# Chunk decays of a state-space mixer: one product with ones for all chunks, instead of one read of a broadcast tile per chunk

## The chip, the cores and the metric

The kernel runs on one core of a Trainium2 chip. The time is the device time of one execution in microseconds (us), and the time before is the median of three executions. A profile is one further execution, recorded by the hardware profiler; its span, from the first to the last recorded instruction, is a little shorter than the time of that execution.

A core has five engines that run side by side, each with its own queue of instructions that it works off in order: TensorE (PE in the profile; its weight loads are listed apart as PEld), VectorE (DVE), ScalarE (ACT), GpSimd (POOL) and SyncE (SP), which here only issues DMA transfers. An instruction waits on semaphores for what it needs, and everything behind it on its engine waits with it.

## What is computed

One layer of a hybrid decoder on 1024 tokens with 16 learned meta tokens ahead of them, width 1024. Three mixers work in parallel on the same normalised input (stick-breaking attention, a Mamba-2 state-space mixer, latent attention), their outputs go through one output product, and a SwiGLU feed-forward block follows. The change touches only the state-space mixer, and in it the decays. Its part of the reference:

```python
X = (xh * dt[..., None]).reshape(b, nc, BLOCK, G, J, P)
dA = (dt * a).reshape(b, nc, BLOCK, G, J)
Acs = jnp.cumsum(dA, axis=2)
...
decay = jnp.exp(Acs[:, :, -1:] - Acs)
states = jnp.einsum('bclgn,bclgjp->bcgjpn', Bc, X * decay[..., None])
chunk_decay = jnp.exp(Acs[:, :, -1])

def step(carry, inp):
    cd, st = inp
    return carry * cd[..., None, None] + st, carry
...
y_off = jnp.einsum('bclgn,bcgjpn->bclgjp', Cc, prev) * jnp.exp(Acs)[..., None]
```

There are 16 heads in two groups of 8. The tokens fall into 9 chunks: chunk 0 holds the 16 meta tokens, chunks 1 to 8 hold 128 tokens each. For every chunk and head, `chunk_decay` is the exponential of the sum of dA over the chunk, and `decay` is the exponential of that sum less the running sum at each token.

## The kernel before

All operands are float32, but most products are taken as three products of a rounded part and a rest (`hi`, `lo`). The kernel is one long stream of such products: input projections and stick-breaking attention come first, with the convolution units of the state-space mixer between the heads; then the state-space chunks (the SSD stage) together with the latent projections; then latent attention, the gate units, the output product and the feed-forward block. The order of instructions on each engine isn't that of the text: the program is built with `TileContext(nc, schedule_with_timeline_sim=True)`, so a planner lays it down beforehand by a simulated timeline, starting from the order of the text, from marks such as `tc.high_priority` and from `tc.issue_after`. Work of independent parts is interleaved in this way: while the SSD stage runs, TensorE also gets the dense products of the latent projections (L145 to L147 in `dense_fm`, and L896 to L898).

**Where the running sums are made.** `running_sums` (L465) is called once, early in the second pair of attention heads. One product of the upper-triangular `tri` with `d1` (= dt·a, 128 tokens by 9 chunks × 16 heads) gives the running sums of all chunks at once (L468); VectorE copies them into `AT` (L469). Three rounds of transposes then turn them into rows (`acs`) that are stored in device memory as `s_sum` [9 chunks, 16 heads, 128 tokens], by SP (L479 for chunk 0, L482 for the others).

**Where they are used.** `ssd_chunk(c)` (L751) is called for c = 0 to 8. It loads `bc` (L756) and `xs` (L757) through SP, transposes `xs` and multiplies it by dt on the way out of PSUM (`X`, L769, VectorE). Then, for each of the two groups of 8 heads:

- SP loads `R` [128, 8, 128]: each head's row of running sums, copied to all 128 partitions (L786). The pool keeps 4 such tiles.
- ScalarE makes `cd`, the chunk decay, from the last column of `R` (L788); VectorE subtracts `AT` from that last column into `dec` (L789), and ScalarE takes its exponential (L799). Chunk 8 needs neither, as no state follows it.
- For c > 0, ScalarE makes `ea` (L793, two instructions) and `L` (L795, eight instructions, and L804) from `R`; VectorE multiplies `L` by the masked product of B and C (`cbm`, L808; L809).
- GpSimd multiplies `X` by `dec` into `Xd` (L800); TensorE makes the new state contribution `sps` from it (L817); GpSimd multiplies the state `S` by `cd` (L821) and VectorE adds `sps` (L824).
- TensorE makes `yo` from the old state (L813) and `yd` from `L` and `X` (L829). VectorE multiplies `ea` by `yo` (L814), GpSimd adds it to `y` (L834), VectorE adds `yd` (L835).

The tiles of this stage lie in the pool `p2`, which takes over space that stick-breaking attention used before; `AT`, `DT` and `tri` lie in `keep`, which lives longer. Other instructions that the text below meets: the eviction `lat` of a latent unit (L529), its squares and their sum (L517, L518), and the split of a weight in `load_w` (L132 on ScalarE, L134 on GpSimd).

Of the kernel before, what the change touches and what calls it, by code (L numbers as in the profile page):

```python
# [11 lines left out]
F32 = mybir.dt.float32  # L12
F32R = mybir.dt.float32r
BF16 = mybir.dt.bfloat16
AF = mybir.ActivationFunctionType
ALU = mybir.AluOpType
# [7 lines left out]
META = 16  # L24
# [35 lines left out]
def tile_hybrid_block(ctx: ExitStack, tc: tile.TileContext, a: dict):  # L60
    nc = tc.nc
    act, dve, pool, pe, sp = nc.scalar, nc.vector, nc.gpsimd, nc.tensor, nc.sync
# [36 lines left out]
    s_sum = dram.tile([9, 16, 128], F32, name="s_sum")  # L99
# [8 lines left out]
    ones = const.tile([128, 128], F32, name="ones")  # L108
# [71 lines left out]
    tp = tp_st.enter_context(tc.tile_pool(name="tp", bufs=2, space=PSUM))  # L180
# [6 lines left out]
    keep = hn_stack.enter_context(tc.tile_pool(name="keep", bufs=1))  # L187
    AT = keep.tile([128, 9, 16], F32, name="AT")
# [228 lines left out]


    dx = keep.tile([128, 9 * 16], F32, name="dx")

    def step_sizes():
        NC = 9 * 16
# [42 lines left out]
    def running_sums(d1):  # L465
        NC = 9 * 16
        pt = tp.tile([128, 512], F32, tag="tp", name="acum")
        pe.matmul(pt[:, :NC], tri, d1, start=True, stop=True)  # L468
        dve.tensor_copy(AT.rearrange("p b h -> p (b h)"), pt[:, :NC])  # L469

        for i, (t0, n) in enumerate(CH_ALL):
            acs = fill_tile("craw" if i == 2 else "cacc", "acs")[:16]
            pt = tp.tile([128, 512], F32, tag="tp", name="acst")
            for b in range(3 * i, 3 * i + 3):
                b0, w = BLOCKS[b]
                pe.transpose(pt[:16, b0 - t0 : b0 - t0 + w], AT[:w, b, :], ident[:w, :w])
            act.copy(acs[:, :n], pt[:16, :n])
            if i == 0:
                sp.dma_start(s_sum[0, :, :META], acs[:, :META])  # L479
            nb = min(3, n // 128)  # L480
            src = acs[:, n - 128 * nb : n].rearrange("h (b t) -> h b t", b=nb)
            sp.dma_start(s_sum[3 * i + 3 - nb : 3 * i + 3].rearrange("b h t -> h b t"), src)  # L482
# [166 lines left out]
    for i, (q0, qn) in enumerate(((0, 256), (256, 384), (640, 384))):  # L649
        c0, n = CH_ALL[i]  # L650
# [91 lines left out]
    with ExitStack() as st:  # L742
        la = st.enter_context(tc.tile_pool(name="la", bufs=1, side="right", reuse_waits="tile"))
        p2_st = ExitStack()
        p2 = p2_st.enter_context(tc.tile_pool(name="p2", bufs=2, side="right", reuse_waits="tile"))
        yps = st.enter_context(tc.tile_pool(name="yps", bufs=4, space=PSUM, reuse_waits="tile"))
        dsk = p2.tile([128, 8], F32, bufs=1, name="dsk")
        sp.dma_start(dsk, a["d_skip"])
        S = [p2.tile([128, 512], F32, bufs=1, name=f"S{g}") for g in range(2)]

        def ssd_chunk(c):  # L751
            n = META if c == 0 else 128
# [10 lines left out]
            for g in range(2):  # L763
                gs = slice(512 * g, 512 * (g + 1))
                hs = slice(8 * g, 8 * g + 8)
                pt = tp.tile([128, 512], F32, tag="tp", name="xtp")
# [11 lines left out]
            for g in range(2):  # L778
                gs = slice(512 * g, 512 * (g + 1))
                hs = slice(8 * g, 8 * g + 8)  # L780
                cd = p2.tile([128, 8], F32, tag="cd", name="cd")
                dec = p2.tile([128, 8], F32, tag="dec", name="dec")
                L = p2.tile([128, 8, 128], F32, tag="L", name="L")
                ea = p2.tile([128, 4, 128], F32, tag="yt", bufs=1, name="ea")
                R = p2.tile([128, 8, 128], F32, tag="R", bufs=4, name="R")
                sp.dma_start(R[:, :, :n], s_sum[c, hs, :n].partition_broadcast(128))  # L786
                if c < 8:
                    act.activation(cd, R[:, :, n - 1], AF.Exp)  # L788
                    dve.tensor_tensor(dec[:n], R[:n, :, n - 1], AT[:n, c, hs], op=ALU.subtract)  # L789
                if c > 0:  # L790
                    for e in range(2):
                        half = slice(64 * e, 64 * e + 64)
                        act.activation(ea[half], R[half, e::2, :], AF.Exp)  # L793
                    for h in range(8):
                        act.activation(  # L795
                            L[:, h, :], R[:, h, :], AF.Relu, scale=-1.0, bias=AT[:, c, 8 * g + h : 8 * g + h + 1]
                        )
                if c < 8:
                    act.activation(dec[:n], dec[:n], AF.Exp)  # L799
                    pool.tensor_tensor(  # L800
                        heads(Xd[:n, gs]), heads(X[:n, gs]), dec[:n].unsqueeze(2).to_broadcast([n, 8, 64]), op=ALU.mult
                    )
                if c > 0:
                    act.activation(L, L, AF.Exp, scale=-1.0)  # L804
                    pcb = tp.tile([128, 512], F32, tag="tp", name="cbp")
                    pe.matmul(pcb[:, :128], bc[:, g, :], bc[:, 2 + g, :], start=True, stop=True)
                    cbm = p2.tile([128, 128], F32, tag="cbm", name="cbm")
                    dve.tensor_tensor(cbm, pcb[:, :128], tri, op=ALU.mult)  # L808
                    dve.tensor_tensor(L, L, cbm.unsqueeze(1).to_broadcast([128, 8, 128]), op=ALU.mult)  # L809
                    yo = yps.tile([128, 512], F32, tag="y", name="yo")  # L810
                    for j in range(4):
                        ts = slice(128 * j, 128 * (j + 1))
                        pe.matmul(yo[:, ts], S[g][:, ts], bc[:, 2 + g, :], start=True, stop=True)  # L813
                    dve.tensor_tensor(ea, ea, yo.rearrange("p (j t) -> p j t", j=4), op=ALU.mult)  # L814
                if c < 8:
                    sps = yps.tile([128, 512], F32, tag="y", name="sps")
                    pe.matmul(sps, btok[:n, g * 128 : (g + 1) * 128], Xd[:n, gs], start=True, stop=True)  # L817
                    if c == 0:
                        dve.tensor_copy(S[g], sps)
                    else:  # L820
                        pool.tensor_tensor(  # L821
                            heads(S[g]), heads(S[g]), cd.unsqueeze(2).to_broadcast([128, 8, 64]), op=ALU.mult
                        )
                        dve.tensor_tensor(S[g], S[g], sps, op=ALU.add)  # L824
                if c > 0:
                    yd = yps.tile([128, 512], F32, tag="y", name="yd")
                    for h in range(8):
                        hh = 8 * g + h
                        pe.matmul(  # L829
                            yd[64 * (h % 2) : 64 * (h % 2) + 64, 128 * (h // 2) : 128 * (h // 2 + 1)],  # L830
                            X[:, hh * 64 : (hh + 1) * 64], L[:, h, :], start=True, stop=True,
                        )
                    yg = y[:, 4 * g : 4 * g + 4]
                    pool.tensor_tensor(yg, yg, ea, op=ALU.add)  # L834
                    dve.tensor_tensor(yg, yg, yd.rearrange("p (j t) -> p j t", j=4), op=ALU.add)  # L835
# [82 lines left out]
        for c0, n in CH_SHORT:  # L918
            c = slice(c0, c0 + n)
# [839 lines left out]
```

## Time and profile before

| | |
|---|---|
| median of 3 runs | 1741.38 us (1738.69 to 1743.46) |
| the profiled execution | 1737.8 us |
| its span | 1736.0 us |
| SSD stage in it | about 465 to 592 us |

In a row of the groups of instructions stand the line, the engine, the operation, what it writes and reads with the shapes, the count, and then: busy us in total, mean ns of one, and the idle time of the engine just before them with what ended most of it. In the timeline a row begins with the start and the length in us, and the bracket at its end says how long the engine had been idle and on what it had waited. In the view of waits the numbers are the total in us, how many times, and the longest.

### The profile page before, as it was taken

How to read it: one execution, taken by the hardware profiler on the slowest of the kernel's cores; microseconds unless marked ns; L12 is line 12 of the kernel's file. 1: busy time of each engine (PE TensorE's matmuls, PEld its weight loads, DVE VectorE, ACT ScalarE, POOL GpSimd, SP SyncE). 2: the span in 40 equal slices, each digit the busy share in tenths (PEclk: the TensorE clock that was granted, in tenths of full speed). 3: DMA queues.
4: the chain of work that ended last, by engine and by line, in shares of the span. 5: the costliest groups of instructions: out<-in, count | busy, mean ns of one | idle time of the engine just before them, and what ended most of it. 6: DMA issues, size and time to landing. Idle time of an engine off the chain costs nothing.

```text
span 1736.0 us, 26095 instructions
## 1 busy us (share of the span) xinstructions
PE 1681.3 (97%) x9529; PEld 1471.2 (85%) x9529; DVE 1154.7 (67%) x1726; ACT 844.6 (49%) x1763; POOL 735.3 (42%) x525
## 2 busy tenths in 40 slices
PE   8899999999998999999999999999999999999998
PEld 7889999999987789998888878778888888878887
DVE  7677568778587544556576556966666666688644
ACT  7465466556577627776454325422222322343333
POOL 3544335243578447563231445635554555200012
PEclk9999999999999999999999999999999999999999
DMA  4222222122566655348222352222322233999602
GB/s 164 72 73 66 82 81 88 39 83 71 173 213 170 211 203 153 113 122 285 62 80 75 94 178 73 71 100 92 113 93 97 93 101 110 329 395 370 234 1 97
DMA packets 150133, 230.90 MB, mean 133 GB/s; under 512 B 27043, under 2 KB 86597, under 8 KB 150005
## 3 DMA queue, kind: packets, MB, share of 16 engines
q1 hardware_dynamic: 130608, 213.67, 38.1%
q10 hardware_dynamic: 19396, 15.56, 3.0%
q8 instruction: 75, 1.23, 0.3%
q14 instruction: 54, 0.43, 0.1%
HBM read 166.07 MB, written 63.10 MB: 132 GB/s over the span
## 4 chain that ended last, share of the span: by engine, by line
PE 72%; DVE 7%; DMA 6%; issue 2%; POOL 2%; ACT 1%; SPq 1%; DVEq 0%; ACTq 0%; POOLq 0%
PE d_ps L145 8%; PE d_ps L147 8%; PE d_ps L146 8%; PE b_ps L1269 7%; PE b_ps L1271 7%; PE b_ps L1270 7%; PE b_ps L1554 2%; PE b_ps L1555 2%; PE b_ps L1553 2%; PE ptg L326 2%; DMA raw<-in_w_down_dram 1%; PE pv L305 1%; PE ptg L328 1%; PE pv L304 1%; PE sc_ps L979 1%
## 5 line engine op out<-in xcount | busy, mean ns | idle before, releaser
L145 PE MATMUL d_ps<-hnh,whi 128*128 128x384 f32 (+6 forms) x744 | 246.5, 331 | 3.6 <-DVE KS L607 2.4
L147 PE MATMUL d_ps<-hnl,whi 128*128 128x384 f32 (+6 forms) x744 | 246.6, 331 | 0.0
L146 PE MATMUL d_ps<-hnh,wlo 128*128 128x384 f32 (+6 forms) x744 | 245.8, 330 | 0.0
L134 POOL TENSOR_TENSOR wlo<-wraw,whi 128x1024 fp32r<-128x1024 f32 (+1 forms) x57 | 137.3, 2408 | 200.7 <-ACT whi L132 200.2
L145 PEld LDWEIGHTS d_ps<-hnh,whi 128*128 128x128 f32 (+1 forms) x744 | 140.1, 188 | 7.8 <-ACT vs L582 1.7
L147 PEld LDWEIGHTS d_ps<-hnl,whi 128*128 128x128 f32 (+1 forms) x744 | 140.1, 188 | 3.1 <-issue 0.8
L146 PEld LDWEIGHTS d_ps<-hnh,wlo 128*128 128x128 f32 (+1 forms) x744 | 140.1, 188 | 2.3
L1270 PE MATMUL b_ps<-T,wl 128*128 128x512 f32 x352 | 139.1, 395 | 1.3 <-POOL wl L1101 1.3
L1271 PE MATMUL b_ps<-T,wh 128*128 128x512 f32 x352 | 138.7, 395 | 1.3 <-DVE T L1101 1.3
L1269 PE MATMUL b_ps<-T,wh 128*128 128x512 f32 x352 | 139.1, 396 | 0.0
L312 DVE TENSOR_TENSOR pl<-ptg,ph 128x512 fp32r<-128x512 f32 (+1 forms) x160 | 99.8, 628 | 53.1 <-ACT ph L311 51.9
L696 DVE TENSOR_TENSOR_SCAN cm<-cm,sb_mask 128x144 f32<-128x144 f32 (+3 forms) x64 | 107.5, 1687 | 29.1 <-issue 18.8
L1100 ACT CAST op<-raw 128x1024 fp32r<-128x1024 f32 x69 | 71.1, 1050 | 110.3 <-PE d_ps L1555 65.4
L1101 DVE TENSOR_TENSOR op<-raw,op 128x1024 fp32r<-128x1024 f32 x69 | 84.1, 1229 | 40.5 <-ACT op L1100 40.4
L311 ACT CAST ph<-ptg 128x512 fp32r<-128x512 f32 (+1 forms) x160 | 85.6, 542 | 44.2 <-PE ptg L328 23.4
L132 ACT CAST whi<-wraw 128x1024 fp32r<-128x1024 f32 (+1 forms) x57 | 58.8, 1032 | 68.8 <-PE d_ps L147 35.1
L1101 POOL TENSOR_TENSOR wlo<-raw,whi 128x1024 fp32r<-128x1024 f32 x18 | 45.0, 2499 | 109.7 <-ACT whi L1100 109.7
L1101 POOL TENSOR_TENSOR wl<-raw,wh 128x512 fp32r<-128x512 f32 x46 | 75.5, 1648 | 30.2 <-ACT wh L1100 30.2
L1107 POOL TENSOR_TENSOR tt<-tt 128x512 f32<-128x512 f32 (+1 forms) x8 | 8.1, 1015 | 187.6 <-ACT tt L1625 187.4
L1104 DVE TENSOR_TENSOR raw<-raw 128x512 f32<-128x512 f32 x58 | 58.5, 1016 | 42.0 <-DMA raw<-in_w_gate_dram 37.3
L1100 ACT CAST wh<-raw 128x512 fp32r<-128x512 f32 x88 | 53.2, 616 | 65.9 <-PE b_ps L1271 65.8
L1270 PEld LDWEIGHTS b_ps<-T,wl 128*128 128x128 f32 x352 | 66.5, 189 | 17.3 <-POOL wl L1101 1.6
(431 smaller groups left out, 5117.8 us busy)
## 6 DMA issues: line engine op xcount, KB each, us to landing
raw<-in_w_down_dram SPq DMA_DIRECT2D x99, 256.0 KB, 5.3
s_hops<-gs SPq DMA_DIRECT2D x63, 256.0 KB, 2.0
raw<-s_hops SPq DMA_DIRECT2D x63, 256.0 KB, 5.4
raw<-in_w_gate_dram SPq DMA_DIRECT2D x22, 512.0 KB, 3.7
raw<-in_w_up_dram SPq DMA_DIRECT2D x22, 512.0 KB, 4.3
R<-s_sum SPq DMA_DIRECT2D x16, 512.0 KB, 4.7
wraw<-in_w_o_dram SPq DMA_DIRECT2D x16, 512.0 KB, 3.7
wraw<-in_w_xbc_dram SPq DMA_DIRECT2D x12, 512.0 KB, 4.0
```

The costliest lines, as they stand in the source:

```text
L134: pool.tensor_tensor(lo[:, :cols], raw[:, :cols], f32(hi[:, :cols]), op=ALU.subtract)
L145: pe.matmul(ps[:m, :n], wh, mh, start=(kt == 0), stop=False)
L146: pe.matmul(ps[:m, :n], wl, mh, start=False, stop=False)
L147: pe.matmul(ps[:m, :n], wh, ml, start=False, stop=(kt == nkt - 1))
L311: act.copy(ph[:, :n], pt[:, :n])
L312: dve.tensor_tensor(pl[:, :n], pt[:, :n], f32(ph[:, :n]), op=ALU.subtract)
L696: dve.tensor_tensor_scan(rev, rev, sb_mask[:, T - n_all :][:, ::-1], 1.0, ALU.mult, ALU.max)
L1100: act.copy(hi, value)
L1101: eng.tensor_tensor(lo, value, f32(hi), op=ALU.subtract)
L1269: pe.matmul(banks[j], hi[:, ks], UH[u][k], start=start and k == 0, stop=False, skip_group_check=skip)
L1270: pe.matmul(banks[j], lo[:, ks], UH[u][k], start=False, stop=False, skip_group_check=skip)
L1271: pe.matmul(banks[j], hi[:, ks], UL[u][k], start=False, stop=stop and k == 3, skip_group_check=skip)
```

## The change

The sum over each chunk is no longer read from the last column of the broadcast tile. `running_sums` makes it for all chunks at once with a product of a matrix of ones with `d1` (every partition then holds the same sum), and puts beside it that sum less the running sums. At the start of the SSD stage one exponential makes all chunk decays and all decays to the chunk's end (`decay`), and `cd` and `dec` become views of it. Chunk 0 then needs no `R`, so its two loads and the store of its row go; `R` keeps 3 tiles instead of 4. `SUMS` and `decay` take 1152 bytes of each partition.

```diff
+    SUMS = keep.tile([128, 2, 9 * 16], F32, name="SUMS")
...
         dve.tensor_copy(AT.rearrange("p b h -> p (b h)"), pt[:, :NC])
+        pt = tp.tile([128, 512], F32, tag="tp", name="asum")
+        pe.matmul(pt[:, :16], ones[:META], d1[:META, :16], start=True, stop=True)
+        pe.matmul(pt[:, 16:NC], ones, d1[:, 16:], start=True, stop=True)
+        dve.tensor_copy(SUMS[:, 0], pt[:, :NC])
+        pool.memset(SUMS[:, 1, :16], 0.0)
+        for rows, c in ((slice(0, META), slice(0, 16)), (slice(0, 128), slice(16, NC))):
+            dve.tensor_tensor(
+                SUMS[rows, 1, c], SUMS[rows, 0, c], AT.rearrange("p b h -> p (b h)")[rows, c], op=ALU.subtract
+            )
...
             act.copy(acs[:, :n], pt[:16, :n])
-            if i == 0:
-                sp.dma_start(s_sum[0, :, :META], acs[:, :META])
...
+        decay = p2.tile([128, 2, 9, 16], F32, bufs=1, name="decay")
+        act.activation(decay.rearrange("p e b h -> p e (b h)"), SUMS, AF.Exp)
...
-                cd = p2.tile([128, 8], F32, tag="cd", name="cd")
-                dec = p2.tile([128, 8], F32, tag="dec", name="dec")
+                cd, dec = decay[:, 0, c, hs], decay[:, 1, c, hs]
...
-                R = p2.tile([128, 8, 128], F32, tag="R", bufs=4, name="R")
-                sp.dma_start(R[:, :, :n], s_sum[c, hs, :n].partition_broadcast(128))
-                if c < 8:
-                    act.activation(cd, R[:, :, n - 1], AF.Exp)
-                    dve.tensor_tensor(dec[:n], R[:n, :, n - 1], AT[:n, c, hs], op=ALU.subtract)
                 if c > 0:
+                    R = p2.tile([128, 8, 128], F32, tag="R", bufs=3, name="R")
+                    sp.dma_start(R, s_sum[c, hs].partition_broadcast(128))
...
                 if c < 8:
-                    act.activation(dec[:n], dec[:n], AF.Exp)
                     pool.tensor_tensor(
```

## The prediction

> **What bounds the kernel now.** First the page's head and its busy line, then the table of windows around the one stretch that uses the changed tiles (columns: window, length, busy us and count of TensorE, its weight loads, VectorE, ScalarE, GpSimd, then granted clock, DMA share, GB/s).
>
> ```profile
> span 1736.0 us, 26095 instructions
> PE 1681.3 (97%) x9529; PEld 1471.2 (85%) x9529; DVE 1154.7 (67%) x1726; ACT 844.6 (49%) x1763; POOL 735.3 (42%) x525
> ...
> 465.00:592.00 127.00, 118.35 (x856) 98.14 (x856) 94.28 (x121) 101.72 (x255) 95.23 (x68) 0.97 0.66 199
> ...
> 530.00:540.00 10.00, 7.42 (x50) 5.63 (x47) 7.67 (x11) 8.73 (x25) 9.60 (x8) 0.83 0.75 213
> ...
> 550.00:560.00 10.00, 7.64 (x66) 6.16 (x61) 8.36 (x10) 6.84 (x18) 10.00 (x8) 0.94 0.67 175
> 560.00:570.00 10.00, 10.00 (x71) 8.04 (x70) 6.22 (x11) 8.57 (x24) 7.62 (x7) 0.89 0.46 136
> ```
>
> TensorE is busy 97% of the span, so a change pays only where TensorE stands idle. The SSD stage is 465 to 592 us. There TensorE is idle 127 − 118.35 = 8.65 us, and its clock was granted below full in three slices: 10 × (0.17 + 0.06 + 0.11) = 3.4 us lost. The other three engines are 74 to 80% full, each waiting for the others in a ring. The ring's waits touching the change, in the view of waits for 460 to 600 us, the lines of that stage, and the tile view of dec (min/median/max ns):
>
> ```profile
> ACT dec L799 <- DVE dec L789: 15.4, 9, 4.1
> ...
> L788 ACT ACTIVATE cd<-R 128x8 f32<-128x8 f32 x16 | 3.3, 209 | 2.9 <-POOL S L821 1.6 <-DMA R<-s_sum 1.0
> ...
> L789 DVE TENSOR_TENSOR dec<-R,AT 128x8 f32<-128x8 f32 x14 | 10.5, 750 | 2.8 <-POOL Xd L800 2.7
> ...
> L799 ACT ACTIVATE dec<-dec 128x8 f32<-128x8 f32 x14 | 2.9, 204 | 13.2 <-DVE dec L789 13.2
> ...
> L809 DVE TENSOR_TENSOR L<-L,cbm 128x1024 f32<-128x1024 f32 x16 | 30.6, 1911 | 1.1 <-ACT L L804 0.8
> ...
> L789 DVE TENSOR_TENSOR dec<-R,AT x16: 147/840/1039, 470.8 to 558.3; 128x8 f32<-128x8 f32 x14, 16x8 f32<-16x8 f32 x2
> ```
>
> ScalarE stands 15.4 us waiting for a subtraction of 8 columns that needs 0.15 us at best and takes 0.84 us at the median. So dec is an expensive trifle, but its price to the kernel is only what reaches TensorE.
>
> **The change, part by part.**
>
> *Removed in the stage.* ScalarE loses the 16 cd of 0.209 us (3.3 us) and 16 dec exponentials of about 0.2 us (3.2 us), and the 15.4 us of waiting. VectorE loses the 16 subtractions, some 10.8 us. GpSimd's Xd (L800) now needs only X; before it also needed the R load, L789 and L799. All are off TensorE, so I follow each idle piece of TensorE back in the timeline:
>
> ```profile
> 470.97 0.31 ACT L799 ACTIVATE dec<-dec 16x8 f32<-16x8 f32 x2 [2.18 <-DVE dec L789]
> 471.18 0.45 ACT L529 COPY lat<-d_ps 128x384 f32<-128x384 f32 x1
> 471.69 0.44 PE L145 MATMUL d_ps<-hnh,whi 128*128 128x384 f32 x1 [1.01 <-ACT lat L529]
> ...
> 488.19 2.04 POOL L821 TENSOR_TENSOR S<-S,cd 128x512 f32<-128x512 f32 x1
> ...
> 489.25 1.00 DVE L789 TENSOR_TENSOR dec<-R,AT 128x8 f32<-128x8 f32 x1
> ...
> 490.99 1.10 PE L817 MATMUL sps<-Xd,btok 128*128 128x512 f32 x2 [0.59 <-DVE ea L814]
> ...
> 527.58 1.12 PE L817 MATMUL sps<-Xd,btok 128*128 128x512 f32 x2 [1.77 <-POOL Xd L800]
> ...
> 528.73 1.04 DVE L789 TENSOR_TENSOR dec<-R,AT 128x8 f32<-128x8 f32 x1
> ...
> 530.61 1.13 PE L813 MATMUL yo<-bc,S 128*128 128x128 f32 x8 [0.34 <-DVE y L835]
> ...
> 531.75 1.00 DVE L789 TENSOR_TENSOR dec<-R,AT 128x8 f32<-128x8 f32 x1
> ...
> 534.10 1.33 PE L817 MATMUL sps<-Xd,btok 128*128 128x512 f32 x2 [2.24 <-DVE ea L814]
> ...
> 553.22 0.99 DVE L789 TENSOR_TENSOR dec<-R,AT 128x8 f32<-128x8 f32 x1
> ...
> 557.84 0.33 PE L768 MATMUL xtp<-identr,xs 128*128 128x128 f32 x1 [2.36 <-DVE cbm L808]
> ```
>
> At 471.69 TensorE waits 1.01 us for an eviction queued on ScalarE behind the dec exponential: all of it goes. At 490.99 the 0.59 us is the tail of a 1.00 us dec ahead of ea: it goes. At 530.61 the 0.34 us goes with the dec of 528.73. At 534.10, 2.24 us follow two dec on VectorE (1.04 and 1.00): I take 2.0. At 557.84 one dec of 0.99 stands two instructions ahead in VectorE's queue: 0.99. At 527.58 the wait is GpSimd's own queue, not dec: I take 0 (at most 1.77). Sum 1.01 + 0.59 + 0.34 + 2.0 + 0.99 = **4.9 us**. Half of the 8.65 us of idle going should take half of the lost clock with it, **1.7 us** (ends: 0 and 3.4).
>
> The dec at 489.25 ended at 490.25, with GpSimd's S product (488.19 + 2.04 = 490.23): VectorE's small subtraction is held until GpSimd's instruction is over. The Trainium skill, "SBUF — State Buffer", section "Who interferes with whom", says that a VectorE instruction with two SBUF inputs and a GpSimd instruction that reads SBUF share a port, and the second one to issue blocks until the first is done. The trace agrees with that row. It speaks against the change: the multiply or add that stands next in VectorE's queue has to wait for the same GpSimd instruction, so only the bare 0.147 us per dec would be saved, 16 × 0.147 = 2.4 us, instead of 10.8. The next instructions here that read PSUM (ea, X, y) would pass; L809, both inputs in SBUF, would not. That is the rival "wait inherited".
>
> *The SP queue and DMA.* Chunk 0's two R loads go, and R has 3 slots instead of 4.
>
> ```profile
> 463.72 2.12 SPq L786 DMA_DIRECT2D R<-s_sum  x2
> ...
> 467.31 1.34 SPq L786 DMA_DIRECT2D R<-s_sum  x2
> ...
> L793 ACT ACTIVATE ea<-R x32: 613/627/634, 473.1 to 588.5; 64x512 f32<-64x512 f32 x32
> ...
> DMA to landing us min/median/max: 3.5/4.6/5.7
> ...
> SPq L786 <- ACT ea L793: 31.9, 7, 7.5
> ```
>
> Chunk 1's loads were issued at 467.31 behind 2.12 us of issuing for chunk 0, so they go out 2.1 us earlier. TensorE has other products to run there; beyond the 1.01 us counted I take 0 (ends 0 and −1). Three slots: the 16 groups read R from 473.1 to 588.5, 7.4 us apart (115.4 / 15.5). A slot freed by one group is needed three groups later, so a load has two groups, 14.8 us, for its landing of at most 5.7. R itself is not late. But SP already stands 31.9 us in front of R slots and holds all that is queued behind; this is the rival "three slots".
>
> *Added near 208 us.* Two products with ones, a copy from PSUM, a memset and two subtractions.
>
> ```profile
> L468 PE MATMUL acum<-d,tri x2: 285/286/286, 208.0 to 208.1; 128*128 128x144 f32 x2
> L469 DVE COPY AT<-acum x1: 308/308/308, 208.4 to 208.4; 128x144 f32<-128x144 f32 x1
> ...
> L462 DVE TENSOR_TENSOR d<-DT,acol 128x144 f32<-128x144 f32 x1 | 0.3, 309 | 0.0
> ...
> 213.33 0.41 DVE L319 TENSOR_TENSOR pm<-ptm,pm 16x256 fp32r<-16x256 f32 x1 [4.61 <-ACT pm L318]
> ...
> 205.00:210.00 5.00, 5.00 (x45) 5.00 (x44) 1.71 (x6) 1.27 (x3) 1.94 (x2) 1.00 0.34 102
> 210.00:215.00 5.00, 4.83 (x38) 3.83 (x37) 1.06 (x2) 3.62 (x7) 3.00 (x2) 1.00 0.30 76
> ```
>
> VectorE: a copy of 0.308 and two subtractions of at most 0.309: 0.93 us into a gap of 4.61 us; cost 0, or 0.93 if the gap were gone. GpSimd's memset (16 columns; no row, so 0 to 1 us as an Xd) falls where GpSimd is 49% busy: 0. TensorE is full here, so its new work counts: the 144-column product shows two records of 0.286 starting 0.12 us apart; a 16- and a 128-column product make four such records, **+0.45 us** (ends 0.25 and 1.15). One store and its issue on SP go (0.3 us); taken as 0.
>
> *Added at the stage's start.* One exponential of 128x288 on ScalarE.
>
> ```profile
> L804 ACT ACTIVATE L<-L 128x1024 f32<-128x1024 f32 x16 | 16.8, 1050 | 0.2
> ...
> 460.63 0.42 SPq L748 DMA_DIRECT2D dsk<-in_d_skip_dram  x1
> ...
> 473.62 2.04 POOL L800 TENSOR_TENSOR Xd<-X,dec 16x512 f32<-16x512 f32 x2
> ...
> 440.00:460.00 20.00, 20.00 (x140) 19.75 (x139) 5.60 (x10) 9.66 (x21) 6.77 (x6) 1.00 0.31 95
> ```
>
> Below L804's 1.05 and above a cd's 0.21 us; near 0.43, as it is a quarter of the columns. ScalarE is half idle from 440 to 460: cost 0. The wait that it adds, for space in p2, is over when the first load into that pool (dsk) is issued, at 460.6 us; the first Xd came at 473.6.
>
> Sum: −4.9 − 1.7 + 0.45 = **−6.2 us**. The profiled execution took 1737.8 (span 1736.0), so 1731.6; the median of three runs shown is 1741.38, 3.6 higher, and the runs to come are measured like it: **1735.2 us**.
>
> **The rivals.**
>
> *Wait inherited.* VectorE's stall passes to L809 and to GpSimd's ring, which the change leaves alone (GpSimd 95.23 of 127 us busy, then the fullest but one). Then only 471.69's 1.01 us and the 0.34 and 0.59 go, 1.9 − 0.45 = 1.5: 1739.9 us. For it: 1.77 of the idle is GpSimd's already, and dec ends with GpSimd's product. Against: ea, after dec in three of the pieces, reads PSUM.
>
> *Whole stage tightens.* With the 15.4 us wait out of ScalarE's queue, the ring turns faster and nearly all idle (8.65) and clock (3.4) come back, less 0.45: −11.6, 1729.8 us; hidden stalls inside TensorE's modelled ends could add some. For it: weight loads are 98.14 / 127 = 77% busy in the stage, and 19.75 / 20 = 99% just before. Against: the stage's products with 512 columns need fewer loads for the same time. The Trainium skill ("Perfetto Trace Analysis", section "Identifying the Most-Contended Engine") holds that weight-load time measures TensorE's room better than matmul busy time; taken literally the stage would shrink to about 98.14 / 0.99 = 99 us, 28 less, 1713 us. I give that 0.03, for the column reason.
>
> *Three slots (slower).* Each engine's order is laid down by a planner before the run. If on SP it leaves an R load ahead of the next chunk's xs or a weight load, SP waits one group longer there (7.4 us), and xtp, X and Xd of that chunk, or the dense work that fills TensorE, start late. One such place is covered by other work (SP has waits of up to 7.5 us now); two that TensorE feels cost 14.8 − 6.2 = +8.6: 1750 us. It decides once filler is short, as at 530 to 560 us. For it: those 31.9 us on SP. Against: chunk 0's loads are gone, so the first wait comes no sooner.
>
> *The change doesn't do what it says.* If Xd still came last because X (xtp on TensorE, then VectorE) is what it waits for, 1741 us. Counted with the inherited wait.
>
> **How the numbers follow.** About 0.3% (5.2 us) is what a measurement tells from no change. Forecast, −3 to −9 us: 0.38. Whole stage: 0.14, the literal weight-load reading 0.03. Inherited wait or nothing gained, −3 to +4: 0.27. Three slots, with what else a changed order costs: 0.18. Faster by over 0.3%: 0.17 and 0.27 of the forecast's 0.38, **0.44**; slower by over 0.3%: of the 0.18 nearly all, **0.17**; within: **0.39**. The range, 1725 to 1746, takes in the tightened stage and half of the slower case.
>
> **What would show it.** No L788, L789, L799; VectorE about 10 and ScalarE about 6 us less in the stage; the gaps before 471, 491 and 534 gone; the stage shorter; clock nearer 1.0 at 530 to 570. Wrong, if L809's mean (1.91 us now) grows by what dec lost, if SP's wait for R slots passes 32 us with xs landing late, or if TensorE's idle comes back after 592.

## The result: 0.22% slower, and the profile after

Over 20 runs the changed kernel took 1745.16 us at the median (1741.65 to 1748.63), the kernel before 1742.48 beside it. The ratio is 1.0022, 95% interval 1.0014 to 1.0029: slower, by a little, where a gain of 6.2 us, to 1735.2 us, was predicted. (The quotient of the two medians is 1.0015; the ratios here and below are the recorded ones, not quotients of medians.) The profiled execution took 1743.84 us.

First the page's head and busy line of the changed kernel, then its windows over the SSD stage (columns as before). Line numbers are some lines higher than before: L814 is before's L809, L799 its L793, L839 its L834, L779 its L769, L507 its L499, L704 its L696.

```profile
span 1741.8 us, 26052 instructions
PE 1681.1 (97%) x9533; PEld 1469.8 (84%) x9533; DVE 1137.6 (65%) x1713; ACT 840.0 (48%) x1732; POOL 732.2 (42%) x526
```

```profile
465.00:592.00 127.00, 117.89 (x863) 96.85 (x863) 79.81 (x105) 96.84 (x223) 92.83 (x68) 0.99 0.65 200
530.00:540.00 10.00, 10.00 (x87) 8.36 (x85) 6.07 (x7) 3.41 (x8) 5.65 (x4) 1.00 0.41 129
540.00:550.00 10.00, 7.26 (x49) 5.17 (x48) 6.63 (x10) 9.91 (x24) 8.12 (x8) 0.83 0.85 247
550.00:560.00 10.00, 8.50 (x65) 6.73 (x66) 4.52 (x9) 8.11 (x22) 10.00 (x8) 1.00 0.58 170
560.00:570.00 10.00, 9.17 (x77) 6.90 (x75) 6.96 (x10) 6.29 (x14) 8.53 (x7) 1.00 0.43 133
```

The work that the change removes is gone: in the stage VectorE has 14.5 us less (94.28 to 79.81), ScalarE 4.9 and GpSimd 2.4. TensorE has gained nothing from it: 127 − 117.89 = 9.1 us idle, against 8.65. The next two fences are TensorE's waits between 460 and 600 us (us in total, times, longest), before and after:

```profile
PE sps L817 <- DVE ea L814: 2.8, 2, 2.2
PE xtp L768 <- DVE cbm L808: 2.4, 1, 2.4
...
PE d_ps L145 <- ACT lat L529: 1.0, 1, 1.0
```

```profile
PE cbp L811 <- DVE X L779: 2.9, 2, 2.5
PE sps L822 <- ACT btok L787: 1.6, 2, 1.4
PE sps L822 <- POOL Xd L805: 1.4, 1, 1.4
PE d_ps L901 <- ACT vtok L905: 1.3, 2, 1.0
PE yd L834 <- DVE L L814: 1.1, 2, 0.8
```

The idle pieces that the prediction followed back to dec are gone, and others of the same total stand in their place. What holds the ring now shows in the changed kernel's lines of the stage, and in SP's waits:

```profile
L814 DVE TENSOR_TENSOR L<-L,cbm 128x1024 f32<-128x1024 f32 x16 | 27.5, 1718 | 1.5 <-ACT L L809 1.0
...
L799 ACT ACTIVATE ea<-R 64x512 f32<-64x512 f32 x32 | 20.0, 626 | 24.5 <-POOL y L839 21.8 <-DMA R<-s_sum 2.5
```

```profile
SPq L796 <- ACT ea L799: 64.6, 12, 11.6
```

ScalarE's wait for y ahead of `ea`, in the views of waits from 460 to 600 us, before and after:

```profile
ACT ea L793 <- POOL y L834: 1.1, 3, 0.5
```

```profile
ACT ea L799 <- POOL y L839: 21.8, 7, 6.1
```

ScalarE waited 15.4 us for dec before, and 1.1 us ahead of `ea`. Now it waits 21.8 us ahead of `ea` for GpSimd's y sum. The pool keeps one `ea` tile, and a group can't write it until GpSimd has added the group before to y (L839). The largest of TensorE's new gaps can be followed in the timeline of the changed kernel (start, length, and in brackets the idle time before and what ended it):

```profile
532.43 1.90 POOL L770 TENSOR_TENSOR y<-xs,dsk 128x1024 f32<-128x1024 f32 x1 [3.08 <-DVE S L829]
534.28 2.25 POOL L839 TENSOR_TENSOR y<-y,ea 128x512 f32<-128x512 f32 x1
...
536.57 1.27 ACT L799 ACTIVATE ea<-R 64x512 f32<-64x512 f32 x2 [6.14 <-POOL y L839]
...
538.75 0.52 ACT L525 ACTIVATE sq<-lat 128x384 f32<-128x384 f32 x1 [0.41 <-ACT lat L537]
...
539.42 1.01 POOL L526 TENSOR_TENSOR grow<-grow,sq 128x384 f32<-128x384 f32 x1 [1.92 <-ACT sq L525]
540.38 1.04 POOL L826 TENSOR_TENSOR S<-S,decay 128x512 f32<-128x512 f32 x1
541.46 0.69 DVE L829 TENSOR_TENSOR S<-S,sps 128x512 f32<-128x512 f32 x1 [2.90 <-POOL S L826]
542.06 0.68 DVE L779 TENSOR_TENSOR X<-xtp,DT 128x512 f32<-128x512 f32 x1
...
542.80 0.49 PE L811 MATMUL cbp<-bc 128*128 128x128 f32 x2 [2.54 <-DVE X L779]
```

GpSimd's y sum ends at 536.5; ScalarE, 6.14 us idle, makes ea and only then the latent eviction and its squares; GpSimd waits for those squares with the state product S queued behind; VectorE waits for S with X behind it; TensorE waits 2.54 us for X. Here one removed wait has become another of the same ring.

The second place is one that the prediction never looked at. It lies ahead of the stage: all that the change does there is to drop a 1 KB store near 208 us and to add five small instructions beside it (a sixth, the memset, ran at 3.0 us). The windows from 230 to 460 us, of the kernel before and of the changed one:

```profile
230.00:460.00 230.00, 229.91 (x1537) 221.66 (x1537) 168.61 (x237) 136.59 (x309) 93.62 (x69) 1.00 0.24 71
```

```profile
230.00:460.00 230.00, 226.81 (x1508) 217.98 (x1507) 169.09 (x237) 135.12 (x307) 89.69 (x67) 0.99 0.23 69
420.00:430.00 10.00, 8.10 (x47) 7.86 (x46) 9.79 (x12) 5.57 (x13) 6.05 (x3) 0.83 0.28 73
```

TensorE loses 3.1 us there, in two stalls that the kernel before doesn't have, and its clock fell to 0.83 around the second, 10 × 0.17 = 1.7 us more. The stalls come again in every program with this early order (TensorE busy 226.7 to 226.8 us), the fall of the clock doesn't: `store_first` below, with the same order on TensorE, had 1.00 from 420 to 430 us. The timeline of the changed kernel at the second one:

```profile
420.12 1.27 DVE L507 SCALAR_TENSOR_TENSOR cacc<-d_ps,cw,cacc 128x384 f32<-128x384 f32 x2
...
421.10 2.40 POOL L134 TENSOR_TENSOR wlo<-wraw,whi 128x1024 fp32r<-128x1024 f32 x1 [1.38 <-ACT whi L132]
...
421.46 3.68 DVE L704 TENSOR_TENSOR_SCAN cm<-cm,sb_mask 128x784 f32<-128x784 f32 x1
...
425.07 0.58 DVE L507 SCALAR_TENSOR_TENSOR cacc<-d_ps,cw,cacc 128x384 f32<-128x384 f32 x1
...
425.80 0.47 PE L145 MATMUL d_ps<-hnh,whi 128*128 128x388 f32 x1 [1.90 <-DVE cacc L507]
```

A convolution chunk needs a chain of three multiply-adds on VectorE (L507, into the tile `cacc`; they read TensorE's product out of PSUM, the memory that it writes to, and so free a bank of it). Here a scan of stick-breaking attention stands between the second and the third, and it takes 3.68 us. The same scan in the kernel before also parts a chain, and costs half:

```profile
427.99 0.62 DVE L499 SCALAR_TENSOR_TENSOR cacc<-d_ps,cw,cacc 128x384 f32<-128x384 f32 x1
428.52 1.78 DVE L696 TENSOR_TENSOR_SCAN cm<-cm,sb_mask 128x784 f32<-128x784 f32 x1
430.22 0.59 DVE L499 SCALAR_TENSOR_TENSOR cacc<-d_ps,cw,cacc 128x384 f32<-128x384 f32 x1
```

In the changed kernel GpSimd's weight split began 0.36 us ahead of the scan and ran to 423.50. The scan ended at 425.14, 1.64 us after that: it was held until GpSimd was done, and the profile counts the holding as busy. The Trainium skill, "SBUF — State Buffer", section "Who interferes with whom", has the rule: a VectorE instruction with two SBUF inputs and a GpSimd instruction that reads SBUF exclude each other, the second one waiting to the end of the first. This trace agrees, with 1.64 us left of the scan after GpSimd's end. At the first stall it is the same: a scan of 3.69 us from 382.28 us on ended 1.65 us after a weight split of 2.40 us that began at 381.92.

So the change altered more than its own lines. Set side by side as lists of lines and shapes, the programs of before and after differ in some 2,650 of TensorE's 9,168 places, from 208 us on; 24 of them come with the added products alone (`sums_only` below).

### The profile page after: what moved, and what is told of

It is laid out like the page before. It is cut to its first block, busy times and chain, and to the rows that moved or that the text cites. A ratio compares the mean times of both kernels' runs of the same rounds, so it can differ in the third digit from the quotient of the medians.

```text
span 1741.8 us, 26052 instructions
## 1 busy us (share of the span) xinstructions
PE 1681.1 (97%) x9533; PEld 1469.8 (84%) x9533; DVE 1137.6 (65%) x1713; ACT 840.0 (48%) x1732; POOL 732.2 (42%) x526
## 4 chain that ended last, share of the span: by engine, by line
PE 75%; DVE 9%; DMA 5%; issue 4%; ACT 3%; POOL 2%; SPq 1%; ACTq 0%; DVEq 0%; POOLq 0%
PE d_ps L145 8%; PE d_ps L147 8%; PE d_ps L146 8%; PE b_ps L1275 7%; PE b_ps L1274 7%; PE b_ps L1276 7%; PE b_ps L1559 2%; PE b_ps L1560 2%; PE b_ps L1558 2%; PE ptg L326 2%; PE ptg L328 1%; PE pv L305 1%; PE pv L304 1%; DVE cm L704 1%; DMA s_y<-y 1%
## 5 line engine op out<-in xcount | busy, mean ns | idle before, releaser
L704 DVE TENSOR_TENSOR_SCAN cm<-cm,sb_mask 128x144 f32<-128x144 f32 (+3 forms) x64 | 108.2, 1696 | 31.9 <-issue 17.9
L1105 ACT CAST wh<-raw 128x512 fp32r<-128x512 f32 x88 | 53.1, 616 | 64.6 <-PE b_ps L1276 64.5
L1276 PEld LDWEIGHTS b_ps<-T,wh 128*128 128x128 f32 x352 | 66.4, 189 | 16.8 <-DVE T L1106 1.6
```

Source lines behind the costliest of these rows:

```text
L704: dve.tensor_tensor_scan(rev, rev, sb_mask[:, T - n_all :][:, ::-1], 1.0, ALU.mult, ALU.max)
L1105: act.copy(hi, value)
L1276: pe.matmul(banks[j], hi[:, ks], UL[u][k], start=False, stop=stop and k == 3, skip_group_check=skip)
```

## The experiments

All ratios are to the kernel before, run on the same chip in the same session. "Order" is each engine's list of instructions as the planner laid it down.

### What in the change costs or pays

**The added products alone** (`sums_only`): the kernel before with the products with ones, their copy, the memset and the two subtractions at 208 us; nothing reads the result.

```diff
+    SUMS = keep.tile([128, 9 * 16], F32, name="SUMS")
...
+        pe.matmul(pt[:, :16], ones[:META], d1[:META, :16], start=True, stop=True)
+        pe.matmul(pt[:, 16:NC], ones, d1[:, 16:], start=True, stop=True)
+        pool.memset(SUMS[:, :16], 0.0)
+        dve.tensor_copy(SUMS, pt[:, :NC])
...
+                SUMS[rows, c], SUMS[rows, c], AT.rearrange("p b h -> p (b h)")[rows, c], op=ALU.subtract
```

> The kernel before plus the products with ones, the copy, the memset and the two subtractions at 208 us; the SSD stage is untouched and doesn't use the sums. Theory 'order': the added steps cost at most the 0.45 us of TensorE, ratio 1.0000 to 1.0005, no wait on cacc at 387 and 426 us. Rival 'added steps': 1.002 to 1.003, with TensorE idle after 208 us.

Measured: 1740.59 us, 1.0005 (0.9993 to 1.0016). Its order is that of before but for 24 places on TensorE, and the two stalls aren't there. By the interval at most 0.16% can be the price of the added work, and the faster kernels below have that work too.

**The store put back** (`keep_store`): the changed kernel with the two removed lines again; nothing reads what they write.

```diff
             act.copy(acs[:, :n], pt[:16, :n])
+            if i == 0:
+                sp.dma_start(s_sum[0, :, :META], acs[:, :META])
```

> The changed kernel with one thing put back: the 1 KB store of chunk 0's row (nobody reads it any more). Theory 'order': without that store the planner laid out VectorE's queue from 208 to 455 us in another way, with scans between the three multiply-adds of a convolution unit, and TensorE waited there (5 us lost between 320 and 440 us). With the store the order up to 455 us is that of the kernel before, so the two waits on cacc at 387 and 426 us go and the time falls by about 5 us, to a ratio of 0.998 to 1.000. Rival 'added steps': the loss comes from the products, copy and subtractions at 208 us, which stay: ratio 1.002, as the changed kernel. Rival 'three slots': the loss is in the SSD stage, ratio 1.002 as well.

Measured: 1728.78 us, 0.9933 (0.9915 to 0.9951). One superfluous 1 KB store makes the changed kernel 0.9% faster, about 15.5 us by the ratios (1.0022 − 0.9933, of 1742), and 0.67% faster than before. The order theory had expected 0.998 to 1.000: the early waits went as it said, but the gain is 8 us or more beyond what it counted. Its windows, and its waits in the stage:

```profile
230.00:460.00 230.00, 229.97 (x1539) 221.85 (x1538) 168.59 (x237) 136.54 (x309) 94.07 (x69) 1.00 0.24 72
465.00:592.00 127.00, 122.40 (x896) 102.97 (x896) 82.80 (x113) 96.06 (x222) 99.20 (x68) 0.99 0.69 213
```

```profile
ACT ea L801 <- POOL y L841: 11.0, 7, 3.8
```

```profile
SPq L798 <- ACT ea L801: 55.7, 12, 7.0
```

The early loss isn't there, and from 465 to 592 us TensorE is busy 4.5 us more than after and 4.1 more than before, with the same VectorE work removed. ScalarE's wait for y is half as long. SP's wait for R slots is nearly as long as in the slow kernel: it doesn't tell the two apart.

Where the time goes over the span shows in the start of two later groups, the last of the stage's products and the first of the output product's stage (tile views, min/median/max ns, first and last start), in before, after and the kernel with the store kept:

```profile
L829 PE MATMUL yd<-L,X x256: 272/273/472, 488.2 to 590.3; 128*64 128x128 f32 x128
...
L1269 PE MATMUL b_ps<-T,wh x352: 389/392/628, 1083.2 to 1500.7; 128*128 128x512 f32 x176
```

```profile
L834 PE MATMUL yd<-L,X x256: 272/273/366, 488.1 to 592.1; 128*64 128x128 f32 x128
...
L1274 PE MATMUL b_ps<-T,wh x352: 389/392/632, 1087.5 to 1505.4; 128*128 128x512 f32 x176
```

```profile
L836 PE MATMUL yd<-L,X x256: 272/273/325, 491.2 to 586.5; 128*64 128x128 f32 x128
...
L1276 PE MATMUL b_ps<-T,wh x352: 388/392/629, 1074.9 to 1492.8; 128*128 128x512 f32 x176
```

After the change the later stage starts 4.3 us late; with the store kept 8.3 us early, of which 3.8 are there at the stage's end. The rest comes between, in the work that the stage had left over; where in it, isn't shown.

**A second ea tile** (`ea2`, and `keep_store_ea2` with the store kept as well):

```diff
-                ea = p2.tile([128, 4, 128], F32, tag="yt", bufs=1, name="ea")
+                ea = p2.tile([128, 4, 128], F32, tag="yt", bufs=2, name="ea")
```

> The changed kernel with two ea tiles instead of one. Theory 'ring moved to ea': in the changed kernel ScalarE waits 21.8 us for GpSimd's y sum because ea has one tile; with two this wait falls under 5 us, the SSD stage gets 3 to 8 us shorter, ratio 0.998 to 1.0005 (the loss of 5 us before the stage stays). Rival 'GpSimd bound': the wait goes on to the next instruction, the stage keeps its length within 1.5 us, ratio 1.0015 to 1.003.

> The changed kernel with the store put back and two ea tiles. If both theories hold the gains add: ratio 0.994 to 0.998. If only the order holds: 0.998 to 1.000. If neither: 1.002.

Measured: 1734.89 us, 0.9970 (0.9956 to 0.9984), and 1731.12 us, 0.9953 (0.9935 to 0.9972). In the changed kernel the second tile, with the order that it brings, is worth half a per cent, more than expected, though ScalarE's wait for y fell to 8.8 us and not under 5. The early stalls stay (TensorE busy 226.82 us between 230 and 460). With the store kept a second tile brings nothing that can be measured. In both pairs TensorE's order changes too, in some 440 and 540 places, so the tile alone isn't priced. SP's wait for R slots falls to 3.7 us in the second, from 55.7, and nothing is gained by that.

### Is it the store, or the order?

**The store on other queues**: in the kernel before from GpSimd (`before_store_pool`), in the changed kernel from ScalarE (`keep_store_act`).

```diff
-                sp.dma_start(s_sum[0, :, :META], acs[:, :META])
+                pool.dma_start(s_sum[0, :, :META], acs[:, :META])
```

> The kernel before, unchanged but for the queue that issues the 1 KB store of chunk 0's row: GpSimd's instead of SP's. VectorE's order in the convolutions comes out as in the changed kernel (14 of 36 chains of three multiply-adds parted by a scan, against 10). Theory 'order': TensorE waits on cacc near 387 and 426 us though no decay was touched, 4 to 6 us lost between 320 and 440 us, ratio 1.002 to 1.004. Rival 'it takes the new sums': no wait there, ratio 0.999 to 1.001.

> The changed kernel with the store put back, but issued from ScalarE's queue; the order in the convolutions is that of the changed kernel (14 chains parted). Theory 'order': the store as such does nothing, so the 5 us between 320 and 440 us stay lost and the ratio is 0.999 to 1.003. Rival 'the store itself' (its transfer, or the row in memory, is what helps): 0.993 as with the store on SP.

Measured: 1740.29 us, 1.0001 (0.9989 to 1.0014), and 1742.12 us, 1.0015 (1.0001 to 1.0030). Both programs have 14 of the 36 convolution chains parted by a scan, like the changed kernel, where before has 10, and both show its two stalls on cacc. With the store on ScalarE TensorE's order is the changed kernel's but for 11 places, and so is the time: a store of its size, issued from elsewhere, doesn't help. The first was a miss: before's program was expected to lose what the two stalls take, and they came, yet its total stayed. Its one profile doesn't show where they were made up: TensorE is busy 133.04 us from 460 to 600 there, against 131.35 in before, but at a granted clock of 0.94 against 0.98 and with 928 recorded products against 935, and the output product's stage still starts 3.3 us late (1086.5 against 1083.2). So the two stalls alone don't tell the time; an order has a price as a whole.

**A store elsewhere on SP, two ways.** `store_end` puts the superfluous store behind the last of the others; `store_first` puts one ahead of the transposes.

```diff
             sp.dma_start(s_sum[3 * i + 3 - nb : 3 * i + 3].rearrange("b h t -> h b t"), src)
+            if i == 2:
+                sp.dma_start(s_sum[0, :, :META], acs[:, :META])
```

```diff
+        sp.dma_start(s_sum[0, :, :16], SUMS[:16, 0, :16])
         for i, (t0, n) in enumerate(CH_ALL):
```

> The changed kernel with one more 1 KB store on SP, of 16 columns of the last rows of running sums, behind the last of the other stores (nothing reads what it writes). In its program the order of VectorE, ScalarE and GpSimd is that of the kernel with chunk 0's store kept, 10 convolution chains parted by a scan; TensorE's and SP's differ from it in two places. Theory (the order decides, wherever the store stands): 0.992 to 0.9955 of the kernel before, no wait of TensorE on cacc between 230 and 460 us. Rival (it is chunk 0's store at its own place that gives SP or the memory a pause): 1.000 to 1.004, like the changed kernel.

> The changed kernel with one more 1 KB store on SP, of 16 columns of SUMS, ahead of the transposes of the running sums (nothing reads what it writes). In its program TensorE, VectorE and GpSimd have the changed kernel's order, 14 chains parted by a scan; ScalarE differs in two places, SP in 17. Theory (the order decides): 1.000 to 1.004, with the waits of TensorE on cacc of about 1.1 and 1.9 us near 386 and 425 us. Rival (any store there is enough): 0.992 to 0.9955.

Measured: 1730.99 us, 0.9937 (0.9919 to 0.9954), and 1743.02 us, 1.0016 (1.0004 to 1.0028). Both times the time was told beforehand from the program's order. Two stores of one size on the same queue, some lines apart in the text, give times 0.8% apart. TensorE's waits on cacc from 230 to 460 us are those of the changed kernel in the second; in the first there are none, and its scan of 784 columns is a short one (timeline):

```profile
PE d_ps L145 <- DVE cacc L508: 3.0, 2, 1.9
```

```profile
428.56 0.62 DVE L509 SCALAR_TENSOR_TENSOR cacc<-d_ps,cw,cacc 128x384 f32<-128x384 f32 x1
429.10 1.78 DVE L706 TENSOR_TENSOR_SCAN cm<-cm,sb_mask 128x784 f32<-128x784 f32 x1
```

### What an R slot is worth

**Four slots** (`r4`) need space (SUMS and `decay` take 1152 bytes of a partition each, 2304 together): the exponential of SUMS is made in place and chunk 8's columns, which nothing reads, are left out. `r3inplace` is the control with three slots.

```diff
-    SUMS = keep.tile([128, 2, 9 * 16], F32, name="SUMS")
+    SUMS = keep.tile([128, 2, 8 * 16], F32, name="SUMS")
...
-        decay = p2.tile([128, 2, 9, 16], F32, bufs=1, name="decay")
-        act.activation(decay.rearrange("p e b h -> p e (b h)"), SUMS, AF.Exp)
+        act.activation(SUMS, SUMS, AF.Exp)
+        decay = SUMS.rearrange("p e (b h) -> p e b h", h=16)
...
-                    R = p2.tile([128, 8, 128], F32, tag="R", bufs=3, name="R")
+                    R = p2.tile([128, 8, 128], F32, tag="R", bufs=4, name="R")
```

> The changed kernel with four R tiles instead of three; for the space the exponential is taken in place and chunk 8's unused columns are left out. Rival 'three slots': SP's 64.6 us of waiting for R slots fall to about 30 and the SSD stage gets 3 to 7 us shorter, ratio 0.998 to 1.000. Theory 'order and single ea': R is never late by more than 2.5 us, so within 2 us of the same kernel with three tiles (r3inplace).

> The changed kernel with the exponential taken in place and chunk 8's unused columns left out, R with three tiles: the control for r4. All theories: within 2 us of the changed kernel, ratio 1.000 to 1.003.

Measured: 1734.32 us, 0.9967 (0.9953 to 0.9981), and 1745.05 us, 1.0027 (1.0012 to 1.0042). So one slot looked worth 10.7 us, more than even the rival "three slots" had said, though SP's wait for slots fell only to 51.2 us and not to 30. The same pair with the store kept (`keep_store_r4`, `keep_store_r3i`):

> The changed kernel with the store of chunk 0's row kept on SP, four R tiles instead of three, and the exponential of SUMS made in place to find the space for the fourth (chunk 8's 16 columns are left out, which nothing reads). Theory (what decides is the planner's order, and with the order that has no wait on cacc before 460 us the ring has slack already): 0.991 to 0.996, no measurable difference from the changed kernel with the store kept (0.993), as a second ea tile made none there. Rival (a fourth R slot is worth some 10 us under any order, as it was with the store gone): 0.986 to 0.989, with TensorE's pieces idle in 460 to 600 down to 3 us.

> The control of the kernel with store, in-place exponential and four R slots: the same with three slots. In its program VectorE, ScalarE, SP and TensorE have the order of the kernel with the store kept, but for one to four places; GpSimd's memset is moved. Theory (order, not space): as with the store kept, 0.991 to 0.9955, so that the fourth slot, with the 378 places of TensorE's order that it changes, costs 0.2 to 0.5%. Rival (the exponential in place, or chunk 8's columns, costs it): as with four slots, 0.9965 to 0.9975.

Measured: 1735.66 us, 0.9969 (0.9957 to 0.9981), and 1730.06 us, 0.9936 (0.9920 to 0.9952). Under the other order the fourth slot **costs** 0.33%, which neither theory had expected. In both pairs the slot also changes TensorE's order, in 371 places and some 380. So no run prices the slot alone; what is measured is the slot with the order that comes with it, and its sign differs between the two early orders.

### Taking ScalarE's wait out of the ring

**ea behind L** (`ea_last`, and `keep_store_ea_last` with the store kept): the two ea instructions are placed behind the exponential of their group's L, so that L doesn't stand behind the wait for y.

```diff
-                    for e in range(2):
-                        half = slice(64 * e, 64 * e + 64)
-                        act.activation(ea[half], R[half, e::2, :], AF.Exp)
...
+                    with tc.issue_after(last_on(ACT)):
+                        for e in range(2):
+                            half = slice(64 * e, 64 * e + 64)
+                            act.activation(ea[half], R[half, e::2, :], AF.Exp)
```

> The changed kernel with the two ea instructions of a group placed behind the exponential that makes that group's L in ScalarE's queue, so that L no longer stands behind ScalarE's wait for GpSimd's y sum of the group before; nothing else is altered, and the store stays out. Theory (the stage lost its gain because ScalarE waits for y inside the ring, through the single ea tile): as much is won as by a second ea tile, 0.994 to 0.999 of the kernel before; ScalarE's wait for y between 460 and 600 us falls below 12 us (21.8 in the changed kernel), TensorE's pieces idle in 460 to 600 fall from 9.5 to about 5 us, and the early waits on cacc of about 1.1 and 1.9 us stay. Rival (the second tile helped because R is let go sooner, not because L was freed): 1.001 to 1.004, since ea is later and so R is let go later; SP's wait for R slots rises above 64.6 us.

> The changed kernel with the store kept on SP and ea placed behind its group's L on ScalarE. Theory (the order is good already): 0.991 to 0.996, the same as with the store alone within the measurement. Rival (ScalarE's wait for y, 11.0 us there, still costs): 0.987 to 0.990.

Measured: 1738.40 us, 0.9991 (0.9978 to 1.0003), and 1729.35 us, 0.9936 (0.9921 to 0.9952). In the first, the wait and the windows:

```profile
ACT ea L810 <- POOL y L840: 14.4, 7, 6.2
```

```profile
230.00:460.00 230.00, 226.82 (x1521) 217.95 (x1519) 169.21 (x237) 135.63 (x307) 90.88 (x68) 1.00 0.23 69
465.00:592.00 127.00, 121.94 (x881) 100.26 (x880) 80.65 (x107) 98.74 (x225) 97.32 (x69) 0.97 0.67 208
```

TensorE is 4 us busier in the stage than after (121.94 against 117.89), as the theory wants, but the wait fell to 14.4 us, not below 12, and the clock was 0.97 where it had been 0.99, 127 × 0.02 = 2.5 us. The gain is 0.3%, just short of what was expected, and TensorE's order changes with the move too, in some 510 places. That ScalarE's wait for y is a large part of the stage's loss is supported, by this and by `ea2`, but not shown apart from the order. With the store kept the move leaves TensorE's order as it was; ScalarE's wait falls from 11.0 to 8.7 us, and nothing is gained.

**The part in the stage alone** (`late_store`): the sums are made at the stage's start from dA formed anew, and the store is kept.

```diff
...
+        SUMS = p2.tile([128, 2, 9 * 16], F32, bufs=1, name="SUMS")
+        dA = SUMS[:, 1]
+        dve.tensor_tensor(
+            dA.rearrange("p (b h) -> p b h", h=16), DT, acol.unsqueeze(1).to_broadcast([128, 9, 16]), op=ALU.mult
+        )
...
```

> The changed kernel with the store kept on SP, and the sums with ones made at the start of the SSD stage from dA formed anew (one more multiply of 144 columns on VectorE), instead of beside the running sums at 208 us. It has the part of the change inside the stage and nothing of the part before it. Theory (the added products cost nothing where they stand, and the gain comes from the stage): 0.992 to 0.996. Rival (what is made at 208 us costs its own time, or there is another order that it brings): the part in the stage alone is better than 0.991; or the work at the stage's start stands in the way of the first chunks: above 0.998.

Measured: 1737.28 us, 0.9977 (0.9967 to 0.9987). A miss, between the two theories: less gain than with the sums at 208 us, where they cost nothing that can be measured. Early, its order has before's 10 parted chains; TensorE's order differs from that of the kernel with the store kept in 403 places. Whether the new order in the stage or the new work at its start takes the 0.4% isn't settled.

### All of them

| kernel | ratio | 95% | chains parted |
|---|---|---|---|
| changed + store kept | 0.9933 | 0.9915 to 0.9951 | 10 |
| same, ea behind L | 0.9936 | 0.9921 to 0.9952 | 10 |
| same, exponential in place | 0.9936 | 0.9920 to 0.9952 | 10 |
| changed + store at the end | 0.9937 | 0.9919 to 0.9954 | 10 |
| changed + store, two ea | 0.9953 | 0.9935 to 0.9972 | 10 |
| changed + store, in place, four R | 0.9969 | 0.9957 to 0.9981 | 10 |
| sums at the stage's start, store | 0.9977 | 0.9967 to 0.9987 | 10 |
| before + added products | 1.0005 | 0.9993 to 1.0016 | 10 |
| changed, in place, four R | 0.9967 | 0.9953 to 0.9981 | 14 |
| changed, two ea | 0.9970 | 0.9956 to 0.9984 | 14 |
| changed, ea behind L | 0.9991 | 0.9978 to 1.0003 | 14 |
| before, store from GpSimd | 1.0001 | 0.9989 to 1.0014 | 14 |
| changed + store on ScalarE | 1.0015 | 1.0001 to 1.0030 | 14 |
| changed + store first | 1.0016 | 1.0004 to 1.0028 | 14 |
| changed | 1.0022 | 1.0014 to 1.0029 | 14 |
| changed, exponential in place | 1.0027 | 1.0012 to 1.0042 | 14 |

The parted chains mark which of the two early orders a program has; they aren't the cause by themselves: before has 10 of them, and TensorE is busy 229.91 of the 230 us there. The change with its variants comes to −0.23 to −0.67% under the one, and to +0.27 to −0.33% under the other. No kernel tried beats the changed one with the store kept by more than the measurement tells.

What carries the argument are the programs that share an order. Three have TensorE's order of the changed kernel in all but at most 11 places (store first, store on ScalarE, exponential in place): with it they lie from 1.0015 to 1.0027, and TensorE is busy 117.89 to 119.39 us from 465 to 592 us. Three have that of the kernel with the store kept in all but at most two (store at the end, exponential in place, `ea` behind L): with it they lie from 0.9933 to 0.9937, at 122.40 to 123.76 us. The other programs, whose orders differ from both in some hundreds of places or more, came out between.

## Why the prediction was wrong

**The step that failed** is "One store and its issue on SP go (0.3 us); taken as 0". A store of its size on ScalarE's queue or ahead of the others gains nothing (1.0015, 1.0016), so its own time isn't the point. But the sum took all other instructions' order as given (a changed order stood only in the price of a rival), and without that store the planner laid down another one from 208 us on. Put back, it saves 15.5 us by the ratios. In the two profiles, whose spans are 12.8 us apart, 3.1 us of it are TensorE's stalls and 1.7 us the clock before 460 us (this one a matter of the single execution), 4.5 us lie between 465 and 592 us, and the rest, some 3.5 us, behind. That the order does it, and not the store, is shown by the programs that share an order. Why the planner decides so at 208 us, and which parts of the order cost what, no run shows. That 1745.16 us lies within the stated 1725 to 1746 us is owed to the width of the range, not to the mechanism of the forecast.

Point by point:

- *Idle pieces of 4.9 us.* The waits on lat, on ea behind dec and on cbm went, as said. With the changed kernel's order others of the same size came; with the store kept, TensorE's idle time in the stage is 127 − 122.40 = 4.6 us, against 8.65, so 4.05 us went where 4.9 were forecast. Some 0.3 us of the 4.9 was counted twice: the dec at 528.73 stands for the piece at 530.61 and again for that at 534.10.
- *Clock, 1.7 us.* No run bears the term out as a consequence of idle time. In the changed kernel's profile the stage's clock is 0.99, against 0.97 before, 127 × 0.02 = 2.5 us; the slices at 530, 550 and 560 us are at full speed, but that at 540 us fell to 0.83, and 420 to 430 us lost another 1.7 us. `store_first` and `keep_store_act`, with nearly the same order, had 0.97 in the stage, and `keep_store_r4` 1.00 with 127 − 118.07 = 8.9 us idle, as much as before.
- *Added products, +0.45 us.* Not contradicted, but too small to be told from nothing: 1.0005, interval −0.07 to +0.16%. One of the two subtractions took 0.82 us where at most 0.31 was said. The exponential took 0.445 us where 0.43 was said:

```profile
L756 ACT ACTIVATE decay<-SUMS x1: 445/445/445, 465.7 to 465.7; 128x288 f32<-128x288 f32 x1
```

- *"Wait inherited".* As it was put, it is not what happened: L809's successor L814 didn't take dec's waiting over, its mean went from 1911 to 1718 ns. Something near it is seen: the wait that went (ScalarE for dec, 15.4 us) made room for one of the same ring (ScalarE for y, 21.8 us). The prediction listed what ScalarE would no longer wait for, and not what stands next in its queue with a single buffer.
- *"Whole stage tightens", 1729.8 us.* Its number is that of the changed kernel with the store kept, 0.9933 of 1742 or 1730, but by luck: its mechanism had nearly all of the stage's 8.65 us idle and 3.4 us of clock come back, and there 4.05 us and 2.5 us did; the stage ended 3.8 us earlier, and the rest came behind it. The literal reading of weight-load time wasn't borne out: with the store kept the stage's weight loads rose to 102.97 of 127 us, and TensorE gained 4 us there, not 28.
- *"Three slots", 1750 us.* The sign came true, the mechanism isn't borne out. SP's wait for R slots doubled (31.9 to 64.6 us) as that rival said, but it is 55.7 us in the kernel that is 0.67% faster, and the fourth slot helps under one order and costs under the other. That rival's chance took in "what else a changed order costs", and this part is what came.

## What to carry to other kernels

Where a planner lays down the order, an edit is the edit plus a new order of everything behind it: compare the two programs' lists first, and time a change together with a neutral twin (here a superfluous 1 KB store) before a per cent is put down to it. When a wait is taken out of a ring of engines, ask which single-buffered tile the same engine reaches next. And an instruction of VectorE whose time has doubled is worth a look at what GpSimd does beside it.

## What the runs showed of the hardware

A scan of 128x784 on VectorE takes 1.78 us alone and 3.68 us when GpSimd's 2.40 us weight split begins 0.36 us ahead of it; the difference is shown as busy time of VectorE, with no wait beside it, and the 1.90 us of TensorE that it costs appear as a wait on the multiply-add behind. In two places this makes up the 3.0 us that TensorE waits on cacc in the changed kernel before 460 us; in the kernel before with its store on GpSimd the same two waits came, and its time stayed (1.0001).
